# One of twelve weight pieces multiplied whole in float32 in the 64-token expert turns

## The chip, the cores and the metric

The kernel runs on one core of a Trainium2 chip. TensorE multiplies, VectorE (DVE in the profile) and ScalarE (ACT) prepare its operands, GpSimd (POOL) does little here, and SyncE (SP) issues the loads. The metric is the time of one execution in microseconds (us), as the median of several.

## The reference

Two layers of a decoder trunk, 256 tokens of width 1024, all in float32. Layer 0 mixes with RWKV-7 and a latent attention and ends in a dense SwiGLU; layer 1 mixes with two attentions and ends in a choice of 2 out of 8 experts. The change touches the experts alone:

```python
def swiglu(t, w_gate, w_up, w_down):
    return (jax.nn.silu(t @ w_gate) * (t @ w_up)) @ w_down

def moe_swiglu(t, router, w_gate, w_up, w_down):
    logits = (t @ router).astype(jnp.float32)
    top_logits, top_idx = lax.top_k(logits, TOP_K)          # TOP_K = 2
    gates = jax.nn.softmax(top_logits, axis=-1)
    combine = jnp.sum(jax.nn.one_hot(top_idx, N_EXPERTS) * gates[..., None], axis=1)
    out = jnp.zeros_like(t)
    for e in range(N_EXPERTS):                              # 8 experts of width 3584
        out = out + combine[:, e:e + 1] * swiglu(t, w_gate[e], w_up[e], w_down[e])
    return out
```

## The kernel before

**Splits.** A product in float32 accuracy is made of fp32r products. `split_raw` turns a float32 weight piece of 128x1024 into two fp32r tiles: `whi` is a rounded copy that ScalarE casts (L192), `wlo` the rest that VectorE subtracts (L193). There are four pairs of `whi`/`wlo` buffers in the expert stage, used in turn, so the fifth split after another takes its buffers and must wait until TensorE has read them.

**Turns.** The experts run in eight turns, "LSLSLSLS". The four experts with the most tokens get L turns of up to 128 tokens, the others S turns of 64. In an L turn the tokens' operand has its own high and low tile, and a product is three matmuls (high x `whi`, low x `whi`, high x `wlo`). In an S turn high and low part of 64 tokens stand side by side in one 128-column operand, so a product is two matmuls (x `whi`, x `wlo`); rows 0 to 63 of the result are those of the high part, rows 64 to 127 those of the low part, and they are added later.

**Blocks.** A turn has seven blocks of 512 of the 3584 hidden columns. A block is `gate_up` (eight pieces: four of the gate, four of the up weights, result `gu`) and `down` (four pieces, accumulated into `Y`, two banks of 512 columns). They are interleaved by one: `gate_up` of a block comes ahead of `down` of the block before it. In the turns of S, `fold` makes the hidden values: `msg` and `mhl` are copies of `gu`, four small transposing matmuls `hT` fold the two halves together, ScalarE applies silu into half of a tile also called `mhl` (L1549), VectorE multiplies (L1554), and `split_to` gives the pair `mhh` that `down` multiplies. These steps are deferred by fixed numbers of pieces (`after` and `tick`); in an ordinary S block the multiplication follows the fourth piece of the next `gate_up` and the split `mhh` the sixth.

**Order.** Each engine runs its instructions in the order in which they are written. `piece` calls `run_ahead`, which splits ahead until four pieces are ready, the current one among them. So the split of a piece is written three pieces ahead of its matmuls.

**Other work in between.** The sums of a turn are added to `h` during the next turn's first two blocks (`combine`: `yh`, `yl`, matmuls `cmb`, four additions L1604 on VectorE). In a turn's fifth and sixth `down` the tokens of the next expert are gathered (`dispatch`): VectorE makes `sel` (L1395, or L1397 for an S turn), TensorE gathers with it (`xT`).

**Loads.** The weights of a block are six loads of 1 MB, each holding two pieces (`weights`, units j = 0 to 5: 0 to 3 for `gate_up`, 4 and 5 for `down`). They go through a ring of sixteen 1 MB places, all issued on SyncE's queue. Three of the places are pairs of half-size `raw` tiles, the rest are `mraw` tiles. A place is free again when its pieces have been read.

The functions that the change touches, and their callers:

Of the kernel before, what the change touches and what calls it, by code (L numbers as in the profile page):

```python
# [28 lines left out]
NFC = DE // 512  # L29
# [9 lines left out]
PLACE = (0, 4, 1, 5, 2, 6, 3, 7)  # L39
KIND = "LSLSLSLS"  # L40
NLARGE = 4

# [66 lines left out]
def _build(tc, nc, es, I, out, dbg, upto):  # L111
# [28 lines left out]
    def ps(shape, name, tag="ps"):  # L140
        return banks[tag].tile(shape, F32, name=name, tag=tag)
# [20 lines left out]
    def load_pieces(src, n, piece, mid=None):  # L162
        raws = []
        for j in range(0, n, piece):
            raw = wraw.tile([128, 1024], F32, name="raw", tag="raw")
            w = min(piece, n - j)
            nc.sync.dma_start(raw[:, :w], src[:, j:j + w])
            raws.append(raw[:, :w])
            if len(raws) == 2 and mid is not None:
                mid()  # L170
        return raws

    def stream(src, n, piece=1024):
        raws = load_pieces(src, n, piece)

        def split(i):
            return split_raw(raws[i])
        return split
# [3 lines left out]
    def split_raw(raw):  # L182
        w = raw.shape[-1]
        p = parts_.pop(0)
        parts_.append(p)
        hi = p.tile([128, 1024], F32R, name="whi", tag="whi")
        lo = p.tile([128, 1024], F32R, name="wlo", tag="wlo")
        split_to(hi[:, :w], lo[:, :w], raw)
        return hi[:, :w], lo[:, :w]

    def split_to(hi, lo, src):
        nc.scalar.copy(out=hi, in_=src)  # L192
        nc.vector.tensor_tensor(out=lo, in0=src, in1=hi.bitcast(F32), op=OP.subtract)  # L193
# [18 lines left out]
    def gain(k, n=D, t=None, o=0, eng=None):  # L212
        g = t if t is not None else b4([128, D], "gain")
        src = I[k]
        (eng or nc.gpsimd).dma_start(g[:, o:o + n],
                                     bass.AP(tensor=src.tensor, offset=src.offset, ap=[[0, 128], [1, n]]))
        return g

    def C(k):
        for offs, t in ((_COFF, cst), (_LOFF, csl), (_KOFF, csk)):  # L220
            if k in offs:
                o, n = offs[k]
                return t[:, o:o + n]
# [9 lines left out]
    def preload(func, after=None):  # L233

        after = eps if after is None else after.bitcast(F32)
        nc.scalar.activation(dummy, after, func, bias=eps, scale=0.0)  # L236
# [38 lines left out]
    half = (slice(0, 512), slice(512, 1024))  # L275
# [291 lines left out]
    with ExitStack() as l0:  # L567
# [129 lines left out]
        Y, bonus, mv = {}, {}, {}  # L697
# [330 lines left out]
    with ExitStack() as l0:  # L1028
# [42 lines left out]
        def a8(shape, name, dt=F32):  # L1071
            return a8p.tile(shape, dt, name=name, tag="a8")
# [3 lines left out]
        t = unp.tile([128, 2, D], F32, name="un")  # L1076
# [16 lines left out]
    with l1:  # L1093
# [91 lines left out]
        def load(src, eng=None):  # L1185
            p = ring.pop(0)
            ring.append(p)
            if p is wraw:
                return stream(src, 2048)
            raw = a8([128, 2048], "mraw") if p is a8p else p.tile([128, 2048], F32, name="mraw", tag="mraw")  # L1190
            (eng or nc.sync).dma_start(raw, src)
            return lambda i: split_raw(raw[:, i * 1024:(i + 1) * 1024])
        early = []

        def load_early():
# [23 lines left out]
    t = unp.tile([128, 2, D], F32, name="un")  # L1219
# [8 lines left out]
    L, m, rank, comb, gm = (rt[:, :, i] for i in range(5))  # L1228
# [93 lines left out]
    def turns():  # L1322
# [25 lines left out]

        nc.vector.tensor_scalar(room, place, NLARGE - 0.5, 64.0, op0=OP.is_lt, op1=OP.mult)
        nc.vector.tensor_scalar(room, room, 64.0, None, op0=OP.add)  # L1350
# [9 lines left out]
    def experts(kinds, late=None, hook=None):  # L1360
# [6 lines left out]
        def after(n, f):  # L1367
            deferred.append([n, f])

        def tick():  # L1370

            for d in list(deferred):
                d[0] -= 1
                if d[0] == 0:
                    deferred.remove(d)
                    d[1]()

        def weights(e, fc, j):
            if late is None or e == 0:
                return I["moe"][e, fc, j]  # L1380
            return I["moe"][ds(turn_reg[e], 1), fc, j].rearrange("o p n -> (o p) n")
# [85 lines left out]
        units = [(0, 0, j) for j in range(4)]  # L1467
        for e in range(len(kinds)):
            for fc in range(NFC):
# [2 lines left out]
                elif e < last:  # L1472
                    units += [(e + 1, 0, j) for j in range(4)]
                units += [(e, fc, j) for j in (4, 5)]
        raws, ready = [(sp, i) for sp in early for i in range(2)], []
        del units[:len(early)], early[:]

        def load_unit(eng=None):
            sp = load(weights(*units.pop(0)), eng)
            raws.extend((sp, i) for i in range(2))  # L1480

        def run_ahead(n=1 + AHEAD):
            while len(ready) < n and (raws or units):
                if not raws:
                    load_unit()
                    if not units:
                        gf[0] = gain("final_norm", t=wraw.tile([128, D], F32, name="raw", tag="raw"), eng=nc.sync)
                sp, i = raws.pop(0)
                ready.append(sp(i))

        def piece():

            run_ahead()
            return ready.pop(0)

        def products(large, terms):

            for o, a, b, start, stop in terms:
                for i, x in enumerate(a if large else (a,)):
                    nc.tensor.matmul(o, lhsT=x, rhs=b[0], start=start and i == 0, stop=False)  # L1500
            for o, a, b, start, stop in terms:
                nc.tensor.matmul(o, lhsT=a[0] if large else a, rhs=b[1], start=False, stop=stop)  # L1502
# [32 lines left out]
        def fold(sums, end):  # L1535

            H = mt.tile([128, 4, 128], F32R, name="mhh")
            t = mt.tile([128, 512], F32, name="mhl").rearrange("p (w f t) -> p w f t", w=2, f=4)
            pt = []

            def turned(w, fs):
                if not pt:
                    pt.append(ps([128, 2, 4, 64], "hT", "hT"))
                for f in fs:
                    nc.tensor.matmul(pt[0][:, w, f, :], lhsT=sums[w][:, f * 128:(f + 1) * 128], rhs=C("fold"),  # L1545
                                     start=True, stop=True)

            def silu():
                nc.scalar.activation(t[:, 0], pt[0][:, 0], AF.Silu)  # L1549
                if end:  # L1550
                    preload(AF.Sqrt)

            def times():
                nc.vector.tensor_tensor(out=t[:, 1], in0=t[:, 0], in1=pt[0][:, 1], op=OP.mult)  # L1554

            def parts():
                split_to(H[:, :, 0:64], H[:, :, 64:128], t[:, 1])
            for i in range(4):
                after(2 if end else 2 + i, lambda i=i: turned(i // 2, range(2 * (i % 2), 2 * (i % 2) + 2)))
            for n, f in zip((3, 3, 4) if end else (7, 8, 10), (silu, times, parts)):  # L1560
                after(n, f)
            return H

        def hidden_T(sgt):
            pt = ps([128, 4, 128], "hT", "hT")
            for f in range(4):
                nc.tensor.transpose(pt[:, f, :], sgt[:, f * 128:(f + 1) * 128], ident)
            hi = mt.tile([128, 4, 128], F32R, name="mhh")
            lo = mt.tile([128, 4, 128], F32R, name="mhl")
            split_to(hi, lo, pt)  # L1570
            return hi, lo

        def down(e, fc, hd, Y, nx, every=0):
            large = kinds[e] == "L"
            turn = nx is not None and kinds[e if fc + 1 < NFC else e + 1] == "L"
            for f in range(4):
                wh, wl = piece()
                if turn and f == (3 if (e, fc) != (last, NFC - 2) else 2):
                    nx = hidden_T(nx)
                x = (hd[0][:, f, :], hd[1][:, f, :]) if large else hd[:, f, :]  # L1580
                products(large, [(Y[q], x, (wh[:, half[q]], wl[:, half[q]]), fc == 0 and f == 0, fc == NFC - 1 and f == 3)
                                 for q in range(2)])
                for _ in range(every):
                    next(side[0], None)
                tick()
            return nx
# [30 lines left out]
        hd = gate_up(0, 0)  # L1617
# [12 lines left out]
        for e in range(len(kinds)):  # L1630
            Y = [ps([128, 512], "Y", "Y") for _ in range(2)]
            for fc in range(NFC):
# [6 lines left out]
                if fc == NFC - 3 and e < last:  # L1639
                    nxt = dispatch(e + 1)  # L1640
                    side[0] = until_parts(nxt)
                    hd = down(e, fc, hd, Y, nx, 2)
                    run(side[0])
                elif fc == NFC - 2 and e < last:
                    side[0] = nxt
                    hd = down(e, fc, hd, Y, nx, 1)
                    run(nxt)
                else:
                    hd = down(e, fc, hd, Y, nx)
# [4 lines left out]

    ring[:0] = [wraw2] * NRAW2 + [a8p]
    moe = experts(KIND, slots1(), gates)
    last = 99
    for n, step in enumerate(out_):
# [147 lines left out]
```

## Time and profile before

| what | value |
|---|---|
| median of 3 runs | 1522.19 us (1521.95 to 1523.29) |
| the profiled execution: its time | 1520.67 us |
| its span, first to last instruction | 1518.7 us |
| mean granted TensorE clock | 0.989 |
| expert stage, first to last `gu` matmul | 560.7 to 1486.3 us |
| busy in the span: TensorE / VectorE / ScalarE | 1435.2 / 1243.8 / 1047.1 us |

The S turns' `down` blocks run from 705.89, 941.54, 1177.12 and 1412.77 us. A row of a timeline gives start, duration, engine, line, operation, output and inputs, shape and count; in brackets stands how long the engine was idle before it and what released it. Matmuls overlap, so their cost is read from starts, not from durations. PEclk is the granted clock as a share of the full one. A row of busy time in a stretch gives the stretch, its length, and for PE, PEld, DVE, ACT and POOL the busy time with the number of instructions.

### The profile page before, as it was taken

How to read it: one execution, taken by the hardware profiler on the slowest of the kernel's cores; microseconds unless marked ns; L12 is line 12 of the kernel's file. 1: busy time of each engine (PE TensorE's matmuls, PEld its weight loads, DVE VectorE, ACT ScalarE, POOL GpSimd, SP SyncE). 2: the span in 40 equal slices, each digit the busy share in tenths (PEclk: the TensorE clock that was granted, in tenths of full speed). 3: DMA queues.
4: the chain of work that ended last, by engine and by line, in shares of the span. 5: the costliest groups of instructions: out<-in, count | busy, mean ns of one | idle time of the engine just before them, and what ended most of it. 6: DMA issues, size and time to landing. Idle time of an engine off the chain costs nothing. (4 is left out here: it accounts for less than half of the span.)

```text
span 1518.7 us, 22486 instructions
## 1 busy us (share of the span) xinstructions
PE 1435.2 (95%) x7781; PEld 1203.5 (79%) x7781; DVE 1243.8 (82%) x1634; ACT 1047.1 (69%) x1440; POOL 86.0 (6%) x154
## 2 busy tenths in 40 slices
PE   7889999999999999999989999989999989999994
PEld 6879888998788888787778887778887778878773
DVE  6786865554586669989989989989989989988995
ACT  6645345444454568878878769878768879777894
POOL 4223110001010010000000000000000000000000
PEclk9999999999999999999999999999999999999998
DMA  8230025557554759889999989999989999998951
GB/s 305 72 109 15 1 98 184 183 188 277 170 189 139 280 188 371 336 345 393 396 368 402 357 331 388 400 380 387 372 332 367 397 399 382 361 373 332 396 233 46
DMA packets 78994, 426.85 MB, mean 281 GB/s; under 512 B 9280, under 2 KB 9552, under 8 KB 43920
## 3 DMA queue, kind: packets, MB, share of 16 engines
q1 hardware_dynamic: 78048, 422.38, 73.8%
q0 software_dynamic: 816, 2.87, 0.6%
q8 instruction: 65, 1.06, 0.3%
q14 instruction: 65, 0.53, 0.1%
HBM read 424.15 MB, written 1.05 MB: 280 GB/s over the span
## 5 line engine op out<-in xcount | busy, mean ns | idle before, releaser
L193 DVE TENSOR_TENSOR wlo<-mraw,whi 128x1024 fp32r<-128x1024 f32 x546 | 645.3, 1221 | 49.4 <-ACT whi L192 43.0
L192 ACT CAST whi<-mraw 128x1024 fp32r<-128x1024 f32 x546 | 559.9, 1050 | 118.5 <-PE Y L1500 54.8
L1500 PE MATMUL gu<-whi,x 128*128 128x512 f32 x1344 | 388.0, 397 | 0.1
L193 DVE TENSOR_TENSOR wlo<-raw,whi 128x1024 fp32r<-128x1024 f32 x242 | 291.3, 1221 | 107.7 <-ACT whi L192 100.6
L192 ACT CAST whi<-raw 128x1024 fp32r<-128x1024 f32 x242 | 250.1, 1043 | 132.6 <-PE acc L197 37.9
L1500 PEld LDWEIGHTS gu<-whi,x 128*128 128x128 f32 x1344 | 248.3, 188 | 52.6 <-DVE x L193 0.4
L1502 PE MATMUL gu<-wlo,x 128*128 128x512 f32 x896 | 282.6, 397 | 3.6 <-DVE wlo L193 2.4
L1502 PEld LDWEIGHTS gu<-wlo,x 128*128 128x128 f32 x896 | 165.0, 188 | 53.1 <-DVE wlo L193 17.8
L1500 PE MATMUL Y<-whi,mhh 128*128 128x512 f32 x448 | 171.3, 422 | 20.9 <-DVE mhh L193 20.5
L1502 PE MATMUL Y<-wlo,mhh 128*128 128x512 f32 x448 | 141.5, 397 | 0.5
L1500 PEld LDWEIGHTS Y<-whi,mhh 128*128 128x128 f32 x448 | 79.1, 190 | 43.8 <-DVE mhh L193 31.3
L1502 PEld LDWEIGHTS Y<-wlo,mhh 128*128 128x128 f32 x448 | 84.2, 190 | 23.0 <-DVE wlo L193 3.5
L196 PE MATMUL cp<-u,whi 128*128 128x256 f32 (+1 forms) x360 | 101.9, 283 | 0.0
L197 PE MATMUL cp<-u,wlo 128*128 128x256 f32 (+1 forms) x360 | 101.8, 283 | 0.0
L198 PE MATMUL cp<-u,whi 128*128 128x256 f32 (+1 forms) x360 | 101.8, 283 | 0.0
L1500 PE MATMUL Y<-whi,mhl 128*128 128x512 f32 x224 | 88.0, 393 | 0.0
L197 PEld LDWEIGHTS cp<-u,wlo 128*128 128x128 f32 (+1 forms) x360 | 68.3, 190 | 0.3
L196 PEld LDWEIGHTS cp<-u,whi 128*128 128x128 f32 (+1 forms) x360 | 68.3, 190 | 0.2
L198 PEld LDWEIGHTS cp<-u,whi 128*128 128x128 f32 (+1 forms) x360 | 68.3, 190 | 0.2
L1500 PEld LDWEIGHTS Y<-whi,mhl 128*128 128x128 f32 x224 | 42.2, 188 | 7.9
L196 PE MATMUL tp<-whi,u 128*128 128x512 f32 x96 | 40.7, 424 | 2.4 <-DVE u L193 2.4
L197 PE MATMUL tp<-whi,u 128*128 128x512 f32 x96 | 39.5, 411 | 2.2 <-DVE u L193 2.2
(425 smaller groups left out, 1977.1 us busy)
## 6 DMA issues: line engine op xcount, KB each, us to landing
mraw<-in_moe SPq DMA_DIRECT2D x272, 1024.0 KB, 7.1
raw<-in_moe SPq DMA_DIRECT2D x126, 512.0 KB, 7.3
raw<-in_ffn_gu SPq DMA_DIRECT2D x44, 512.0 KB, 3.7
raw<-in_w_in SPq DMA_DIRECT2D x38, 512.0 KB, 3.7
raw<-in_ffn_d SPq DMA_DIRECT2D x22, 512.0 KB, 3.5
raw<-in_w_out SPq DMA_DIRECT2D x16, 512.0 KB, 3.7
raw<-in_w_in SPq DMA_DIRECT2D x4, 416.0 KB, 8.6
h<-in_x SPq DMA_DIRECT2D x2, 512.0 KB, 6.0
```

The costliest lines, as they stand in the source:

```text
L192: nc.scalar.copy(out=hi, in_=src)
L193: nc.vector.tensor_tensor(out=lo, in0=src, in1=hi.bitcast(F32), op=OP.subtract)
L196: nc.tensor.matmul(o, lhsT=a[0], rhs=b[0], start=start, stop=False)
L197: nc.tensor.matmul(o, lhsT=a[1], rhs=b[0], start=False, stop=False)
L198: nc.tensor.matmul(o, lhsT=a[0], rhs=b[1], start=False, stop=stop)
L1500: nc.tensor.matmul(o, lhsT=x, rhs=b[0], start=start and i == 0, stop=False)
L1502: nc.tensor.matmul(o, lhsT=a[0] if large else a, rhs=b[1], start=False, stop=stop)
```

## The change

In S turns the second of the four `down` pieces (unit j = 4, half i = 1) isn't split. Its raw float32 tile is TensorE's moving operand, and the stationary operand is the hidden tile before its split, 128x64 float32 (`t[:, 1]`, written at L1554 and until now read by the split alone), which `fold` now returns beside `H`. The product is written to rows 0 to 63 of `Y`. It is one float32 matmul for each half of the columns, in place of two fp32r ones. That piece doesn't count among the four that `run_ahead` keeps split. It happens once in each of the 28 S blocks.

```diff
+WHOLE = (4, 1)
...
             if p is wraw:
-                return stream(src, 2048)
+                pieces = load_pieces(src, 2048, 1024)
+                return lambda i: pieces[i]
...
-            return lambda i: split_raw(raw[:, i * 1024:(i + 1) * 1024])
+            return lambda i: raw[:, i * 1024:(i + 1) * 1024]
...
         def load_unit(eng=None):
-            sp = load(weights(*units.pop(0)), eng)
-            raws.extend((sp, i) for i in range(2))
+            e, fc, j = units.pop(0)
+            raw = load(weights(e, fc, j), eng)
+            raws.extend((raw, i, kinds[e] == "L" or (j, i) != WHOLE) for i in range(2))
 
         def run_ahead(n=1 + AHEAD):
-            while len(ready) < n and (raws or units):
+            while sum(len(r) == 2 for r in ready) < n and (raws or units):
...
-                sp, i = raws.pop(0)
-                ready.append(sp(i))
+                raw, i, parts = raws.pop(0)
+                ready.append(split_raw(raw(i)) if parts else (raw(i),))
...
-            return H
+            return H, t[:, 1]
...
-                wh, wl = piece()
+                w = piece()
...
-                x = (hd[0][:, f, :], hd[1][:, f, :]) if large else hd[:, f, :]
-                products(large, [(Y[q], x, (wh[:, half[q]], wl[:, half[q]]), fc == 0 and f == 0, fc == NFC - 1 and f == 3)
-                                 for q in range(2)])
+                x = (hd[0][:, f, :], hd[1][:, f, :]) if large else hd[0][:, f, :]
+                if len(w) == 2:
+                    products(large, [(Y[q], x, (w[0][:, half[q]], w[1][:, half[q]]), fc == 0 and f == 0,
+                                      fc == NFC - 1 and f == 3) for q in range(2)])
+                else:
+                    for q in range(2):
+                        nc.tensor.matmul(Y[q][0:64], lhsT=hd[1][:, f, :], rhs=w[0][:, half[q]], start=False, stop=False)
```

TensorE, one `down` of an S turn and the start of the `gate_up` behind it, before:

```order
L1500 MATMUL Y<-whi,mhh 128x512 x2
L1502 MATMUL Y<-wlo,mhh 128x512 x2
L1500 MATMUL Y<-whi,mhh 128x512 x2
L1502 MATMUL Y<-wlo,mhh 128x512 x2
L1545 MATMUL hT<-csk,msg 128x64 x2
L1500 MATMUL Y<-whi,mhh 128x512 x2
L1502 MATMUL Y<-wlo,mhh 128x512 x2
L1545 MATMUL hT<-csk,msg 128x64 x2
```

The same place on TensorE in the changed kernel (line numbers have moved by a few):

```order
L1504 MATMUL Y<-whi,mhh 128x512 x2
L1506 MATMUL Y<-wlo,mhh 128x512 x2
L1590 MATMUL Y<-mraw,mhl 64x512 x2
L1549 MATMUL hT<-csk,msg 128x64 x2
L1504 MATMUL Y<-whi,mhh 128x512 x2
L1506 MATMUL Y<-wlo,mhh 128x512 x2
L1549 MATMUL hT<-csk,msg 128x64 x2
```

The second pair of rows on `whi` and `wlo` has become one row of two matmuls on the raw tile; nothing else on TensorE has moved.

VectorE from one `mhh` of the first S turn to the next one, and on to the `sel` of the next L expert, before:

```order
L193 TENSOR_TENSOR mhh<-mhl,mhh 128x4x64
L193 TENSOR_TENSOR wlo<-mraw,whi 128x1024 x10
L1554 TENSOR_TENSOR mhl<-mhl,hT 128x256
L193 TENSOR_TENSOR wlo<-mraw,whi 128x1024 x2
L193 TENSOR_TENSOR mhh<-mhl,mhh 128x4x64
L193 TENSOR_TENSOR wlo<-mraw,whi 128x1024 x3
L1395 TENSOR_SCALAR sel<-iota,route 128x128 x2
```

The same place on VectorE in the changed kernel:

```order
L195 TENSOR_TENSOR mhh<-mhl,mhh 128x4x64
L195 TENSOR_TENSOR wlo<-mraw,whi 128x1024 x9
L1558 TENSOR_TENSOR mhl<-mhl,hT 128x256
L195 TENSOR_TENSOR wlo<-mraw,whi 128x1024 x2
L195 TENSOR_TENSOR mhh<-mhl,mhh 128x4x64
L195 TENSOR_TENSOR wlo<-mraw,whi 128x1024 x2
L195 TENSOR_TENSOR wlo<-raw,whi 128x1024
L1398 TENSOR_SCALAR sel<-iota,route 128x128 x2
```

The ten splits between `mhh` and `mhl` are nine; two splits still stand between `mhl` and the next `mhh`, and three between that and `sel` (the third of them is now that of a later piece, from a `raw` tile).

More of the change, by code (lines that the diff above doesn't have):

```diff
@@ L1474, in experts @@
                 units += [(e, fc, j) for j in (4, 5)]
-        raws, ready = [(sp, i) for sp in early for i in range(2)], []
+        raws, ready = [(raw, i, True) for raw in early for i in range(2)], []
         del units[:len(early)], early[:]
         def load_unit(eng=None):
-            sp = load(weights(*units.pop(0)), eng)
-            raws.extend((sp, i) for i in range(2))
+            e, fc, j = units.pop(0)
+            raw = load(weights(e, fc, j), eng)
+            raws.extend((raw, i, kinds[e] == "L" or (j, i) != WHOLE) for i in range(2))
         def run_ahead(n=1 + AHEAD):
-            while len(ready) < n and (raws or units):
+            while sum(len(r) == 2 for r in ready) < n and (raws or units):
                 if not raws:
```

## The prediction

> **What bounds the kernel now.** I read the page's first part, then the time of each block of the expert stage (one query for busy time in stretches), then the timelines of single blocks, and last the clock. The profiled execution took 1520.67 us, of which the span is 1518.7; the median of the runs shown is 1522.19.
>
> ```profile
> PE 1435.2 (95%) x7781; PEld 1203.5 (79%) x7781; DVE 1243.8 (82%) x1634; ACT 1047.1 (69%) x1440; POOL 86.0 (6%) x154
> ```
>
> Over the whole span TensorE looks like the bound, but the average mixes stages. The change touches only the S turns (experts 1, 3, 5, 7). I cut the first of them into its seven blocks, each from the first `Y` matmul of one `down` to that of the next, and add the end of the last one:
>
> ```profile
> core 0: us, PE busy (x) PEld busy (x) DVE busy (x) ACT busy (x) POOL busy (x), PEclk, DMA share, GB/s
> 705.89:722.75 16.86, 15.45 (x71) 11.57 (x71) 16.86 (x19) 14.65 (x18) 0.00 (x0) 1.00 1.01 403
> 722.75:737.69 14.94, 13.94 (x64) 10.40 (x65) 14.94 (x16) 12.76 (x16) 0.00 (x0) 1.00 0.96 365
> 737.69:751.98 14.29, 13.43 (x65) 10.65 (x65) 14.29 (x15) 13.33 (x17) 0.00 (x0) 1.00 1.02 417
> 751.98:766.27 14.29, 13.43 (x65) 10.64 (x65) 14.29 (x15) 13.33 (x17) 0.00 (x0) 1.00 1.01 418
> 766.27:788.05 21.78, 18.80 (x99) 15.83 (x99) 15.22 (x17) 13.61 (x18) 0.00 (x0) 0.92 0.95 363
> 788.05:804.78 16.73, 16.73 (x80) 13.83 (x81) 16.73 (x18) 14.89 (x20) 0.00 (x0) 1.00 0.98 361
> 804.78:820.44 15.66, 15.66 (x71) 12.79 (x70) 15.66 (x16) 14.05 (x17) 0.00 (x0) 1.00 1.01 419
> ...
> 1487.43:1506.98 19.55, 12.29 (x56) 8.90 (x56) 15.05 (x21) 11.10 (x18) 0.00 (x0) 0.95 0.11 39
> ```
>
> Call the seven P0 to P6. In P0 to P3 VectorE has no idle time and TensorE has gaps, so VectorE sets the pace. In P4 the gathers of the next expert come in and neither is full. In P5 and P6 the other half of the work is already that of an L turn, and TensorE has no gap either. So a change that takes work from VectorE and gives some to TensorE can gain in four blocks of seven, and must be priced block by block.
>
> Inside an ordinary block (P2) TensorE's timeline shows the pieces. I call the four pieces of `down` d0 to d3 and the eight of `gate_up` g0 to g7:
>
> ```profile
> 737.69 0.74 PE L1500 MATMUL Y<-whi,mhh 128*128 128x512 f32 x2 [0.73 <-DVE mhh L193]
> ...
> 738.73 0.63 PE L1500 MATMUL Y<-whi,mhh 128*128 128x512 f32 x2
> ...
> 739.66 0.55 PE L1545 MATMUL hT<-csk,msg 128*128 128x64 f32 x4
> 740.02 0.71 PE L1500 MATMUL Y<-whi,mhh 128*128 128x512 f32 x2
> ...
> 744.14 0.71 PE L1500 MATMUL gu<-whi,x 128*128 128x512 f32 x2
> ```
>
> d0 starts at 737.69 after waiting for `mhh` from VectorE; d1 runs from 738.73 to 739.66, 0.93 us for four matmuls, 0.23 each; d2 starts at 740.02; g1 starts at 744.14, 6.45 us after d0.
>
> **The change, part by part.** It happens once in each of 28 blocks, on d1.
>
> *Taken from VectorE and ScalarE:* one `wlo` and one `whi`. Nine `wlo` back to back take 10.30 us, and one alone 1.22, so one costs (10.30-1.22)/8 = 1.14 us of VectorE. A `whi` is 1.05 us (the ACT rows below).
>
> ```profile
> 752.97 10.30 DVE L193 TENSOR_TENSOR wlo<-mraw,whi 128x1024 fp32r<-128x1024 f32 x9
> ```
>
> *Given to TensorE:* four fp32r matmuls of 512 columns go, two float32 ones come. The trace of before has no float32 matmul of 512 columns; the nearest has 256:
>
> ```profile
> 35.35 0.27 PE L198 MATMUL cp<-ul,whi 128*128 128x256 f32 x1
> 35.46 1.24 PE L629 MATMUL lo<-zwa,lora 128*128 128x256 f32 x5
> L629 PE MATMUL lo<-zwa,lora x16: 377/379/483, 35.5 to 39.5; 128*128 128x256 f32 x16
> ```
>
> L629 leaves 16 records for eight matmuls in the source, so a float32 matmul is two records. Five records take 1.24 us with 0.38 for the last, so they start (1.24-0.38)/4 = 0.215 us apart, against 0.11 for the fp32r one of the same width just ahead (35.35 to 35.46). At twice the columns that is 0.43 a record, 0.86 a matmul, 1.72 for d1. So d1 grows by x = 1.72-0.93 = 0.79 us. Bounds: x = 0 if the four records cost no more than fp32r records of that width, and x = 0.91 if each pass costs a full 0.23 twice over (8 x 0.23 = 1.84). I take 0.79, since L629 is the same kind at half the size. By the Trainium skill, FP8 and Floating Point Precision, section TensorE Precision Notes, true FP32 is four passes through the array; at 0.23 a pass that gives 1.84 for d1, and by it the sum below would be +8.7 us instead of +5.4; L629's records are a little faster than that.
>
> *What the gain meets in P2 and P3.* VectorE would need 14.29-1.14 = 13.15 us. But there is a second loop, through the four `whi`/`wlo` buffers: the split of g5 can't start before TensorE has read `whi` of g1, since it has the same buffer. P4's second half shows this loop alone, with VectorE waiting:
>
> ```profile
> 780.78 0.71 PE L1500 MATMUL gu<-whi,x 128*128 128x512 f32 x2
> ...
> 781.52 1.05 ACT L192 CAST whi<-raw 128x1024 fp32r<-128x1024 f32 x1 [0.33 <-PE gu L1500]
> ...
> 782.61 1.23 DVE L193 TENSOR_TENSOR wlo<-raw,whi 128x1024 fp32r<-128x1024 f32 x1 [0.15 <-ACT whi L192]
> ...
> 783.83 1.23 DVE L193 TENSOR_TENSOR wlo<-mraw,whi 128x1024 fp32r<-128x1024 f32 x1
> ...
> 784.97 0.42 DVE L1554 TENSOR_TENSOR mhl<-mhl,hT 128x256 f32<-128x256 f32 x1
> ...
> 785.30 2.35 DVE L193 TENSOR_TENSOR wlo<-mraw,whi 128x1024 fp32r<-128x1024 f32 x2
> ...
> 787.57 0.42 DVE L193 TENSOR_TENSOR mhh<-mhl,mhh 128x256 fp32r<-128x256 f32 x1
> ...
> 788.05 0.51 PE L1500 MATMUL Y<-whi,mhh 128*128 128x512 f32 x1 [0.58 <-DVE mhh L193]
> ```
>
> g1 at 780.78, its `whi` of the g5 buffer at 781.52, then VectorE in order: g5, g6, `mhl`, g7, d0, `mhh`, and TensorE starts the next d0 at 788.05: 7.27 us after g1's start. Of that row of VectorE work nothing is removed, because the dropped `wlo` (d1) stands behind `mhh`. So this loop takes 6.45+7.27 = 13.72 us in P2 before, hidden under VectorE's 14.29, and 13.72+0.79 = 14.51 after: **+0.22** each.
>
> *P1:* 14.94 now, all of it VectorE. After, VectorE needs 13.80 and the loop (g1 starts at 729.18, 6.43 after d0) 6.43+0.79+7.27 = 14.49: **-0.45**.
>
> *P0* has the sums of the L expert before it:
>
> ```profile
> 708.59 0.71 PE L1500 MATMUL Y<-whi,mhh 128*128 128x512 f32 x2
> 709.41 0.74 PE L1502 MATMUL Y<-wlo,mhh 128*128 128x512 f32 x2
> ...
> 713.11 0.71 PE L1500 MATMUL gu<-whi,x 128*128 128x512 f32 x2
> ...
> 714.35 0.39 PE L1603 MATMUL cmb<-yl,sT 128*128 128x512 f32 x1
> ...
> 716.08 0.75 DVE L1604 SCALAR_TENSOR_TENSOR h<-cmb,route,h 128x512 f32<-128x512 f32 x1
> ...
> 729.18 0.71 PE L1500 MATMUL gu<-whi,x 128*128 128x512 f32 x2
> ```
>
> `h` starts at 716.08 because VectorE was busy until then; `cmb` was done at 714.74. After, VectorE is free at 714.94. TensorE is 0.79 later, less 0.40 that d2 loses now to its late `wlo` (d2 to g1 takes 4.52 here and 4.12 in P2, 740.02 to 744.14): `cmb` ends at 715.13, and `h` starts at about 715.2. All behind it moves by **-0.88**. (The split of g5 has its `whi` by 715.3 and is no later.)
>
> *P4:* d0 runs, then TensorE waits 2.40 us for `sel`, which stands on VectorE behind `mhh` and three splits, before (d1, d2, d3) as after (d2, d3, g0). That wait stays. Behind it the chain is TensorE up to g1, and then the 7.27 above: **+0.79**.
>
> *P5 and P6:* TensorE has no gap, and its cover is VectorE's time, which shrinks: **+0.79** each.
>
> *The last S turn* has no next expert: P0 and P1 as above, three blocks of +0.22, and then a tail with d1 twice. There TensorE runs d0, d1, the transposes, and waits for ScalarE and VectorE, in a row:
>
> ```profile
> 1491.32 0.39 ACT L1549 ACTIVATE mhl<-hT 128x256 f32<-128x256 f32 x1 [0.80 <-PE hT L1545]
> ...
> 1495.90 0.73 PE L1500 MATMUL Y<-whi,mhh 128*128 128x512 f32 x2 [2.71 <-DVE mhh L193]
> ```
>
> Both d1 lie on it: 2 x 0.79 = **+1.58**. No cast leaves that row, since one split still stands between the transposes and `mhh`.
>
> *Loads:* a raw tile is freed by TensorE's d1, some 2 us later than by the split. SP's queue waits on freed tiles (562.8 us of waiting, 249 times), not on the DMA, and sixteen tiles of 1 MB are over two and a half blocks of 6 MB, so I cost this at nothing.
>
> ```profile
> SPq L1191 <- DVE wlo L193: 562.8, 249, 9.6
> ```
>
> **Sum.** A turn with a successor: -0.88-0.45+2x0.22+3x0.79 = +1.48; three of them +4.44. The last: -0.88-0.45+3x0.22+1.58 = +0.91. Together **+5.35 us**: 1526.0 on the profiled execution, 1527.5 on the median. In x the sum is 28x-16.8; it turns at x = 0.60.
>
> **The rivals.**
>
> *The relief is handed on (faster).* If splits ran far enough ahead that `mhh` never waited on a buffer, P0 and P1 would gain the whole 1.14, and P2 and P3 would fall to TensorE's own time: 13.62 us (44 matmuls at 0.23, d1 at 1.72, four groups of transposes at 0.45: 0.36 from 739.66 to 740.02 and a slower pair behind), -0.67. Sum: 3 x (-2.28-1.34+2.37) + (-2.28-2.01+1.58) = -6.5, 1515.7. It decides at the wait for `mhh` in P2: gone, this case; there, mine. For it: VectorE is full in P0 to P3. Against it: P4 shows the loop bare. The Trainium skill says so too: Perfetto Trace Analysis, section Identifying the Most-Contended Engine, has one optimize the engine of the highest occupancy first, here VectorE in those blocks; P4's VectorE, at 15.22 of 21.78, is on the chain all the same.
>
> *The clock drops go (no change).* In P4 the wait for `sel` leaves TensorE 1.17 us of work in 3.41, and then the clock is halved for the next 3.41:
>
> ```profile
> 769.87 1.16 PE L1403 MATMUL xT<-sel,un 128*128 128x128 f32 x8 [2.40 <-DVE sel L1395]
> ...
> 767.63:771.04 3.41, 1.17 (x9) 1.17 (x10) 3.41 (x5) 0.68 (x1) 0.00 (x0) 1.00 1.01 420
> 771.04:774.45 3.41, 3.41 (x14) 3.04 (x14) 1.33 (x2) 1.53 (x2) 0.00 (x0) 0.50 1.01 420
> ...
> 1242.08:1245.49 3.41, 3.41 (x14) 3.02 (x13) 1.50 (x2) 1.53 (x2) 0.00 (x0) 0.50 1.01 418
> ```
>
> That costs 1.7 us, three times. First and third lie 471.04 us apart, 138 stretches of 3.413, so they seem to follow a fixed grid, and a shift of the blocks by 1.5 us a pair could move the wait across a grid line. Without two or three of them: 1522.4 to 1524.1. Against it: the wait itself stays as long.
>
> *Float32 is dearer.* x = 0.91 gives 28 x 0.91-16.8 = +8.7: 1530.9.
>
> **How the numbers follow.** A measurement of this kernel can't tell under 0.2%, 3.0 us, from no change. The loop as summed, within 1524.5 to 1530 on its own: 0.58. The clock drops gone: 0.20. Handed on: 0.12. Dearer: 0.10. Slower by over 0.2% (above 1525.2) takes nearly all of the first and the last, 0.63; no change 0.25; faster 0.12. The range leaves out most of the faster case and what lies above the dear one: 1518 to 1531.5.
>
> **What would show it.** P2 at 14.5 us with VectorE no longer full and d0 still waiting for `mhh`; d1 at 1.72; P5 and P6 longer by 0.8 each; P0 and P1 shorter by 0.9 and 0.45. I am wrong if P2 is at 13.6 with no wait for `mhh`, if d1 is near 1.5 or less, or if the halved clock no longer shows.

## The result, and the profile after

The changed kernel takes 1541.51 us in the median (1539.99 to 1543.94, four runs), the kernel before 1522.16 on the same chip: a ratio of 1.0121, 95% interval 1.0107 to 1.0136. It is slower by 19.35 us. The forecast was slower by 5.35 us, with 1531.5 as the upper end. The profiled execution took 1542.74 us, of which its span is 1540.6.

The page's first part of the changed kernel, to be held against the same line of before:

```profile
PE 1464.3 (95%) x7781; PEld 1196.9 (78%) x7781; DVE 1223.2 (79%) x1606; ACT 1022.8 (66%) x1412; POOL 85.8 (6%) x154
```

VectorE's busy time fell by 20.6 us (28 instructions) and TensorE's grew by 29.1 at an unchanged count of matmul records: two float32 matmuls of two records took the place of four fp32r ones. 29.1 over 28 pieces is 1.04 us a piece, where 0.79 had been forecast; it is only a first hint, since the clock is in it too.

The busy time of the first S turn's blocks P0 to P2 and P4 to P6 (P3 is 14.84 like P2), of the end of the last turn, and of P4 in the second S turn (22.95 us in the third):

```profile
core 0: us, PE busy (x) PEld busy (x) DVE busy (x) ACT busy (x) POOL busy (x), PEclk, DMA share, GB/s
708.84:725.22 16.38, 15.95 (x71) 11.49 (x71) 16.00 (x18) 13.80 (x17) 0.00 (x0) 1.00 0.99 399
725.22:740.07 14.85, 14.28 (x65) 10.36 (x65) 14.27 (x15) 11.65 (x15) 0.00 (x0) 1.00 0.98 393
740.07:754.91 14.84, 14.26 (x64) 10.36 (x64) 13.59 (x14) 12.37 (x16) 0.00 (x0) 1.00 1.02 404
...
769.75:793.93 24.18, 21.22 (x99) 15.53 (x99) 13.99 (x16) 12.75 (x17) 0.00 (x0) 0.86 0.81 318
793.93:811.73 17.80, 17.80 (x81) 13.55 (x81) 16.30 (x17) 14.27 (x19) 0.00 (x0) 1.00 0.93 367
811.73:828.52 16.79, 16.79 (x71) 12.42 (x70) 15.45 (x17) 13.20 (x16) 0.00 (x0) 1.00 0.96 374
...
1504.40:1540.60 36.20, 17.43 (x56) 9.15 (x56) 13.54 (x19) 9.77 (x17) 0.00 (x0) 0.72 0.15 48
...
1010.53:1033.49 22.96, 20.01 (x98) 14.62 (x99) 13.99 (x16) 12.74 (x17) 0.00 (x0) 0.93 0.88 335
```

Against before, P0 is shorter by 0.48, P1 by 0.09, P2 and P3 are longer by 0.55 each, P4 by 2.4 in this turn and 1.2 in the others, P5 by 1.07 and P6 by 1.13. In P2 VectorE works 13.59 of 14.84 us: it isn't the bound any more, and the block is longer all the same. The relief was real and bought nothing there.

TensorE's timeline in that P2 shows d0 to d2, g1 and the next d0:

```profile
740.07 0.73 PE L1504 MATMUL Y<-whi,mhh 128*128 128x512 f32 x2 [0.57 <-DVE mhh L195]
740.64 0.62 PE L1506 MATMUL Y<-wlo,mhh 128*128 128x512 f32 x2
741.19 1.93 PE L1590 MATMUL Y<-raw,mhl 128*64 128x512 f32 x4
743.05 0.66 PE L1549 MATMUL hT<-csk,msg 128*128 128x64 f32 x4
743.52 0.71 PE L1504 MATMUL Y<-whi,mhh 128*128 128x512 f32 x2
...
747.64 0.71 PE L1504 MATMUL gu<-whi,x 128*128 128x512 f32 x2
...
754.91 0.73 PE L1504 MATMUL Y<-whi,mhh 128*128 128x512 f32 x2 [0.59 <-DVE mhh L195]
```

d0 to g1 is 747.64 - 740.07 = 7.57 us, against 6.45 before: x = 1.12, and 1.13 by P6 (16.79 - 15.66). From g1 to the next d0 it is 754.91 - 747.64 = 7.27 us, the same as the row taken from P4 of before, and d0 still waits for `mhh`. So the loop of the prediction holds to 0.01 us (7.57 + 7.27 = 14.84), and one number in it was wrong: x. The question for the experiments was where the missing 0.33 us a piece comes from. Three places can be read off: d1 starts 0.55 after the `wlo` group ahead of it, where 0.46 is usual (+0.09); it lasts 743.05 - 741.19 = 1.86 and not the forecast 1.72 (+0.14); and the transposes behind it take 743.52 - 743.05 = 0.47, against 0.36 before (+0.11).

### The profile page after: what moved, and what is told of

It reads as the page before. It is cut to its first block, busy times and chain, and to the rows that moved or that the text cites. A ratio compares the mean times of both kernels' runs of the same rounds, so it can differ in the third digit from the quotient of the medians.

```text
span 1540.6 us, 22379 instructions
## 1 busy us (share of the span) xinstructions
PE 1464.3 (95%) x7781; PEld 1196.9 (78%) x7781; DVE 1223.2 (79%) x1606; ACT 1022.8 (66%) x1412; POOL 85.8 (6%) x154
## 5 line engine op out<-in xcount | busy, mean ns | idle before, releaser
L195 DVE TENSOR_TENSOR wlo<-mraw,whi 128x1024 fp32r<-128x1024 f32 x526 | 630.1, 1223 | 75.1 <-ACT whi L194 62.5
L194 ACT CAST whi<-mraw 128x1024 fp32r<-128x1024 f32 x526 | 542.0, 1051 | 157.8 <-PE Y L1504 94.5
L195 DVE TENSOR_TENSOR wlo<-raw,whi 128x1024 fp32r<-128x1024 f32 x234 | 283.4, 1222 | 115.9 <-ACT whi L194 112.7
L194 ACT CAST whi<-raw 128x1024 fp32r<-128x1024 f32 x234 | 242.2, 1044 | 141.8 <-PE acc L199 37.9
L1504 PE MATMUL Y<-whi,mhh 128*128 128x512 f32 x392 | 153.5, 425 | 16.2 <-DVE mhh L195 15.8
L1506 PE MATMUL Y<-wlo,mhh 128*128 128x512 f32 x392 | 122.8, 395 | 0.1
L1504 PEld LDWEIGHTS Y<-whi,mhh 128*128 128x128 f32 x392 | 68.6, 190 | 40.5 <-DVE mhh L195 26.6
L1506 PEld LDWEIGHTS Y<-wlo,mhh 128*128 128x128 f32 x392 | 73.7, 189 | 18.4 <-DVE wlo L195 1.4
L1549 PEld LDWEIGHTS hT<-csk,msg 128*128 128x128 f32 x224 | 31.3, 190 | 19.4 <-ACT mhl L1528 13.8
L198 PE MATMUL tp<-whi,u 128*128 128x512 f32 x96 | 39.3, 410 | 2.4 <-DVE u L195 2.4
```

The costliest lines, as they stand in the source:

```text
L198: nc.tensor.matmul(o, lhsT=a[0], rhs=b[0], start=start, stop=False)
```

## The experiments

The question of the operand is summed up first; P2 is that of the first S turn. The edits are shown shortened, without the code around them.

| whole piece d1 | stationary columns | kind | P2, us | median, us |
|---|---|---|---|---|
| kernel before | 128 | fp32r, split | 14.29 | 1522.2 to 1522.9 |
| the change (`mhl`) | 64 | float32 | 14.84 | 1541.51 |
| e5 (`mhh`, high half) | 64 | float32 | 14.85 | 1540.07 |
| e9 (`mhh`) | 96 | float32 | 14.50 | 1529.02 |
| e1 (`mhh`) | 128 | float32 | 14.52 | 1527.66 |
| e6 (`mhl`) | 128 | float32 | 14.51 | 1528.89 |
| e2 (`mhh`, high half) | 64 | fp32r, split | 14.29 | 1523.41 |

**e1, 128 columns.** The whole piece is multiplied as float32, but with both parts of the hidden values side by side, as the split pieces have them.

```diff
-nc.tensor.matmul(Y[q][0:64], lhsT=hd[1][:, f, :], rhs=w[0][:, half[q]], ...)
+nc.tensor.matmul(Y[q], lhsT=hd[0][:, f, :].bitcast(F32), rhs=w[0][:, half[q]], ...)
```

> The changed kernel, but the whole piece is multiplied by the 128-column operand (high and low part side by side, read as float32) and written to all 128 rows of Y. In the changed kernel d1 with what it delays takes 1.13 us more than before and not 0.79. Theory A (the number of columns): a 64-column operand isn't loaded under a running 128-column matmul, nor the other way round, and the two switches cost the missing 0.34. Then x is 0.79 here, an ordinary block (P2) 14.51 us, the sum +5.4 us: 1527.5, the drops of the clock at the end included or not, up to 1530. Theory B (the kind): the change from fp32r to float32 and back costs it whatever the columns. Then nothing changes: P2 14.85, 1541.

Measured: 1527.66 us (1521.04 to 1530.36, seven runs) against 1522.85 of before, ratio 1.003 (1.001 to 1.0049). Busy time of P0, P1, P2, of P4 in the three turns with a successor, and of P6:

```profile
707.64:723.66 16.02, 15.60 (x70) 11.86 (x70) 15.91 (x18) 13.79 (x17) 0.00 (x0) 1.00 0.98 396
723.66:738.18 14.52, 13.95 (x65) 10.73 (x65) 14.17 (x15) 11.65 (x15) 0.00 (x0) 1.00 0.99 401
738.18:752.70 14.52, 13.94 (x65) 10.73 (x65) 13.60 (x14) 12.38 (x16) 0.00 (x0) 1.00 1.02 399
767.19:790.87 23.68, 20.73 (x99) 16.05 (x99) 14.00 (x16) 12.74 (x17) 0.00 (x0) 0.86 0.86 336
1005.41:1027.74 22.33, 19.33 (x98) 15.54 (x98) 13.99 (x16) 12.73 (x17) 0.00 (x0) 0.92 0.93 351
1242.19:1263.17 20.98, 17.99 (x98) 14.44 (x98) 13.99 (x16) 12.73 (x17) 0.00 (x0) 1.00 0.99 397
...
808.32:824.77 16.45, 16.45 (x71) 12.79 (x70) 15.45 (x17) 13.19 (x16) 0.00 (x0) 1.00 0.97 381
```

These are the blocks that the prediction forecast for the change itself: P0 15.98, P1 14.49, P2 14.51, P6 16.45. The piece costs x = 16.45 - 15.66 = 0.79. So float32 as such was priced rightly, and the rest lies in what e1 changed: the 64 columns, or the tile that they come from. The three P4 rows show what the clock does by itself (the seven runs go from 1521.04 to 1530.36): 23.68, 22.33 and 20.98 us for the same work, with two halved stretches, one and none.

**e2, 64 columns in fp32r.** The kernel before, with d1 split as ever, but multiplied by the 64 high columns alone; the products with the low part are left out of that piece.

```diff
-x = hd[:, f, :]                      # into Y[q]
+x = hd[:, f, 0:64] if f == 1 else hd[:, f, :]      # into Y[q][0:64] for f == 1
```

> The kernel before, all pieces split, but d1 of each S block multiplies only the 64 columns of the high part (all four matmuls fp32r); left out is the product with the low part in that piece. Theory A: the same switches without any float32, 0.34 us a block, hidden under VectorE in P0 to P3 and seen in P4 to P6 and twice in the tail: 9 x 0.34 + 2 x 0.34 = +3.7, 1526; P6 at 16.0 instead of 15.66. Theory B: no change, 1522, P6 15.66.

Measured: 1523.41 us, ratio 1.0004 (0.9994 to 1.0014). Timeline of P2:

```profile
742.24 0.62 PE L1502 MATMUL Y<-wlo,mhh 128*128 128x512 f32 x2
742.70 0.62 PE L1500 MATMUL Y<-whi,mhh 128*64 128x512 f32 x2
743.16 0.63 PE L1502 MATMUL Y<-wlo,mhh 128*64 128x512 f32 x2
743.63 0.56 PE L1545 MATMUL hT<-csk,msg 128*128 128x64 f32 x4
743.99 0.71 PE L1500 MATMUL Y<-whi,mhh 128*128 128x512 f32 x2
...
742.48 0.37 PEld L1500 LDWEIGHTS Y<-whi,mhh 128*64 128x64 f32 x2
...
743.40 0.65 PEld L1545 LDWEIGHTS hT<-csk,msg 128*128 128x128 f32 x4
```

The groups stand 0.46 to 0.47 apart through both changes of width, and the transposes take 0.36. The two rows of PEld, TensorE's loads of its stationary operand, start 0.22 and 0.23 us ahead of their matmuls. VectorE would hide a small cost in P2; in P6, where TensorE has no gap, the block takes 15.64 us against 15.66 before. So 64 columns cost nothing in fp32r, and the plain form of the theory (the width) falls: it had expected gaps here too. What was left was float32 and 64 columns together, or the `mhl` tile as the source, which e1 had changed along with the width.

**e5 and e6, the two apart.** e5 takes 64 float32 columns from `mhh`, e6 128 from `mhl`.

```diff
 e5: lhsT=hd[0][:, f, 0:64].bitcast(F32)                       # into Y[q][0:64]
 e6: lhsT=hd[1].rearrange("p f t -> p (f t)")[:, 64*f:64*f+128]  # into Y[q]
```

> The changed kernel, but the 64-column float32 operand of the whole piece is taken from the high half of mhh instead of mhl[:, 1]; the low part of the hidden values is left out of that piece. Theory C: float32 matmuls with a stationary operand of 64 instead of 128 columns cost the extra 0.33 us per whole piece, wherever the operand lies. Then x stays at 1.13: d0 to g1 in P2 7.57, P2 14.85, about 1541 us. Theory D: it is the mhl tile as the source (its own wait or its own place) that costs it. Then x = 0.80: d0 to g1 7.25, P2 14.51, about 1527 us.

> The changed kernel, but the float32 operand of the whole piece has 128 columns and still lies in the mhl tile: the 64 columns of piece 1 and the 64 behind them, into all 128 rows of Y, so that products of another piece are added to the low rows. Theory C (64 columns in float32 cost it): P2 14.51, d0 to g1 7.25, about 1527 us, as with 128 columns of mhh. Theory D (the mhl tile costs it): P2 14.85, about 1541 us.

Measured: e5 1540.07 us (ratio 1.0113, 1.0093 to 1.0133), e6 1528.89 (1.0048, 1.0032 to 1.0063). The first fence is P2 of e5, the second of e6, as busy time:

```profile
738.92:753.77 14.85, 14.27 (x65) 10.36 (x65) 13.60 (x14) 12.36 (x16) 0.00 (x0) 1.00 1.02 404
```

```profile
737.70:752.21 14.51, 13.92 (x65) 10.73 (x65) 13.60 (x14) 12.37 (x16) 0.00 (x0) 1.00 1.02 403
```

Theory C (float32 with 64 columns) gave both blocks to 0.01 us; theory D (the `mhl` tile) had them the other way round and falls.

How it costs is seen in the weight loads. First those of the changed kernel around d1, then those of e6:

```profile
740.41 0.42 PEld L1506 LDWEIGHTS Y<-wlo,mhh 128*128 128x128 f32 x2
741.19 0.19 PEld L1590 LDWEIGHTS Y<-raw,mhl 128*64 128x64 f32 x2 [0.36 <-issue]
741.67 0.14 PEld L1590 LDWEIGHTS Y<-raw,mhl 128*64 128x64 f32 x1 [0.29 <-issue]
...
743.05 0.52 PEld L1549 LDWEIGHTS hT<-csk,msg 128*128 128x128 f32 x4 [0.81 <-ACT mhl L1528]
```

```profile
738.26 0.63 PE L1506 MATMUL Y<-wlo,mhh 128*128 128x512 f32 x2
738.50 0.42 PEld L1590 LDWEIGHTS Y<-raw,mhl 128*128 128x128 f32 x2
738.73 1.88 PE L1590 MATMUL Y<-raw,mhl 128*128 128x512 f32 x4
...
740.02 0.19 PEld L1549 LDWEIGHTS hT<-csk,msg 128*128 128x128 f32 x1 [0.24 <-ACT whi L194]
740.44 0.55 PE L1549 MATMUL hT<-csk,msg 128*128 128x64 f32 x4
```

In e6 the load for d1 starts at 738.50, under the matmul before it and 0.23 ahead of its own; the load for the transposes at 740.02, 0.42 ahead. In the changed kernel d1's load starts at 741.19 and the transposes' at 743.05, both in the same moment as their matmuls: on either side of the 64-column piece nothing was loaded ahead. In e5 it is the same (load and matmul of d1 both at 740.04, of the transposes at 741.90), while e1 and e9 load ahead as e6 does, and so does e2 with its 64 columns in fp32r. A 64-column load is short (0.14 us a piece); what was lost is its cover.

By the Trainium skill, TensorE: Matmul & The Clock Gate, section Step-by-step: what each phase is for, TensorE pulls weight loads ahead of running matmuls, with conditions; the rows of e6 agree, those of the change show a place where it doesn't. By the Trainium skill, TensorEngine Tiling (Array Packing), section Key Properties, changing the tiling mode of the array drains TensorE; its section Available Configurations lists a mode of 128x64. The change agrees in sign, at 0.33 us for a switch there and back; e2 doesn't agree, since it changes the width twice at no cost. Why float32 alone loses the cover isn't shown by these runs.

**e9, 96 columns**, to see whether anything below the full width is charged.

```diff
+lhsT=hd[0][:, f, 0:96].bitcast(F32)     # into Y[q][0:96]
```

> The changed kernel with a 96-column float32 operand from mhh (its 64 high columns and 32 of the low ones, the other 32 low ones left out), into 96 rows of Y. If every operand of fewer than 128 columns is charged, P2 is 14.85, d0 to g1 7.57, about 1541 us. If the price comes only with half a stationary array or less, P2 is 14.51, d0 to g1 7.25, about 1527 us. I take the second at 0.6.

Measured: 1529.02 us (ratio 1.003, 1.0008 to 1.0052); busy time of P2:

```profile
740.02:754.52 14.50, 13.92 (x65) 10.63 (x65) 13.60 (x14) 12.36 (x16) 0.00 (x0) 1.00 1.02 407
```

96 columns cost no more than 128. Widths between 64 and 96, and below 64, weren't tried.

**e3, the tail.** The change, with the last turn's last two blocks split as before.

```diff
-raws.extend((raw, i, kinds[e] == "L" or (j, i) != WHOLE) for i in range(2))
+raws.extend((raw, i, kinds[e] == "L" or (j, i) != WHOLE or (e == last and fc > 4)) for i in range(2))
```

> The changed kernel, but the last two blocks of the last turn split all pieces. Theory A with the clock: the tail gets back two pieces of 1.13 and the 2.6 us that the halved clock took behind the last wait for mhh: -4.9, 1536.6. Rival (the clock drop in the tail has nothing to do with the whole pieces): -2.3, 1539.2, with the halved clock still there.

Measured: 1537.63 us (1536.36 to 1540.95, four runs), ratio 1.0099 (1.0075 to 1.0124), 3.9 us below the change. The stretches from the last `down` to the end of the span, and the one halved clock stretch with work in it:

```profile
1504.05:1536.80 32.75, 13.85 (x56) 10.08 (x56) 15.73 (x21) 11.66 (x19) 0.00 (x0) 0.74 0.16 53
...
1513.03:1516.44 3.41, 3.41 (x9) 2.67 (x8) 0.56 (x1) 0.00 (x0) 0.00 (x0) 0.50 0.00 0
```

The tail is 32.75 where the change has 36.20 and before 31.27. The work is that of before again, and it is still 1.48 us longer, with one halved stretch at work in it (the change has two, from 1513.30). So the two whole pieces of the tail and what the clock made of them are about 3.4 us together, and the 1.48 that is left is about what one full stretch at half the clock costs (half of 3.41 is 1.7, an estimate). Neither expectation came out whole: one halved stretch went with the pieces, the other stayed. The interval of the ratio reaches some 4 us to either side, so the time alone wouldn't tell the two apart.

**e4, another piece.** The whole piece is now g6 (the seventh of `gate_up`), with the 128-column tokens' operand, in blocks 2 to 5 alone (counted from 0; their g6 fall in P0 to P3). On VectorE g6 stands inside the row from g1 to `mhh` that closes the loop; d1 stands behind it.

```diff
-WHOLE = (4, 1)
+WHOLE = (3, 0)                          # and only where 2 <= fc <= 5
+if len(pw) == 1:
+    nc.tensor.matmul(a, lhsT=x.bitcast(F32), rhs=pw[0][:, c], start=kb == 0, stop=kb == 7)
```

> The whole piece on 128 columns is not d1 but g6, and only in gate_up of blocks 2 to 5 of an S turn, 16 in all. The dropped split then stands between that of g5 and mhh, inside the loop that the prediction named. Theory (the loop through the buffers decides): the loop is 1.14 shorter, an ordinary block falls to TensorE's own 13.8 us, P0 and P1 gain 1.1 each, P2 and P3 0.45 each: -12.4, 1510. Rival (the place in the block doesn't matter, only how much goes to which engine): P0 -0.88, P1 -0.45, P2 and P3 +0.22, so 4 x -0.89 = -3.6, 1518.6.

Measured: **1505.87 us** (1505.27 to 1507.48, four runs), ratio 0.9892 (0.9872 to 0.9912), faster than both. P0, P1, P2 and P4:

```profile
706.68:723.54 16.86, 15.89 (x70) 11.74 (x70) 16.86 (x19) 14.13 (x17) 0.00 (x0) 1.00 1.01 411
723.54:737.36 13.82, 13.82 (x65) 10.74 (x65) 13.82 (x15) 11.68 (x15) 0.00 (x0) 1.00 1.00 397
737.36:751.12 13.76, 13.76 (x65) 10.78 (x65) 13.48 (x14) 12.39 (x16) 0.00 (x0) 1.00 1.03 418
764.85:784.07 19.22, 17.14 (x100) 14.37 (x99) 14.11 (x16) 13.56 (x17) 0.00 (x0) 1.00 1.01 412
```

P1 and P2 are now TensorE's own time, with no gap left (13.82 of 13.82, 13.76 of 13.76), which is what the rival of the relief handed on had described, at 13.62. P4 is 2.6 us shorter than before, with the clock at 1.00 throughout: the splits run one piece further ahead, so `sel` stands behind two splits and not three, TensorE waits 1.50 us for it and not 2.40, and the clock isn't halved. P0 gained nothing: the splits run one piece ahead there, and d1's takes the freed place ahead of `mhh`. So 1506 instead of the expected 1510 isn't the loop's doing alone: P1 to P3 give some 2.2 us a turn (P3 is 13.73), 8.8 in all, where 8.0 was expected; P0's 4.4 didn't come, and the three P4 brought 7.7 that the expectation didn't have.

**e7, `mhh` earlier.** e1, with the split into `mhh` scheduled one piece earlier, so that on VectorE it stands ahead of d0's split.

```diff
-for n, f in zip((3, 3, 4) if end else (7, 8, 10), (silu, times, parts)):
+for n, f in zip((3, 3, 4) if end else (7, 8, 9), (silu, times, parts)):
```

> As the kernel with 128 columns of mhh (1527.66 us), but the split into mhh is scheduled one piece earlier (7, 8, 9 instead of 7, 8, 10), so that on VectorE it stands ahead of the split of d0 and not behind it. Loop theory: the way from g1 to the next d0 (7.26 us) loses the 1.15 of d0's split, and d0's second half then waits some 0.6 for that split: P2 and P3 about 14.0 instead of 14.51, P5 and P6 (no gap on TensorE) unchanged, about 1521 us in all. Rival, VectorE's or TensorE's sum alone sets P2: no change, 1527 to 1528 us.

Measured: 1523.63 us (1522.21 to 1526.42, ten runs), ratio 1.0007 (0.9997 to 1.0016), 4.0 below e1. P0, P2 and P5:

```profile
707.27:723.68 16.41, 15.34 (x71) 11.86 (x70) 16.28 (x18) 13.51 (x18) 0.00 (x0) 1.00 0.97 401
737.49:751.57 14.08, 13.92 (x65) 10.73 (x64) 13.63 (x14) 12.43 (x16) 0.00 (x0) 1.00 1.01 395
788.39:806.14 17.75, 17.61 (x81) 13.73 (x80) 17.11 (x18) 15.55 (x21) 0.00 (x0) 1.00 0.98 395
```

P2 fell from 14.52 to 14.08 (14.0 was expected), with the same work on both engines; a bound by either engine's sum, the rival, would have left it. What is left is no longer the loop: TensorE works 13.92 of 14.08 us and doesn't wait for `mhh`, only 0.16 for d0's split. P0 grew by 0.39 and P5, forecast as unchanged, by 0.30: what the earlier `mhh` pushes back on VectorE comes late there. In P0 TensorE stands 1.07 us until `yl` is written, and in P5 the `wlo` matmuls of d0 start 0.77 behind its `whi` ones, where 0.46 is usual. Some 4 of the 6.5 us expected were kept.

**e8, one block more.** e4 with g6 whole in blocks 1 to 5.

```diff
-... or (j, i) != WHOLE or not 2 <= fc <= 5
+... or (j, i) != WHOLE or not 1 <= fc <= 5
```

> As the kernel with g6 whole on 128 columns in blocks 2 to 5 (1505.87 us), but in blocks 1 to 5. The piece of block 1 then falls in P0, where VectorE has one split less ahead of mhh: P0 about 15.75 instead of 16.86 in four turns, -1.1 each, 1501.5 us. Rival: TensorE, which carries the sums of the expert before in P0, or the two h additions set its end: P0 at 16.5 or more, 1504.5 to 1506 us.

Measured: **1502.36 us** (1501.43 to 1506.76, four runs), ratio 0.9864 (0.9847 to 0.988). P0:

```profile
710.18:725.87 15.69, 15.59 (x71) 11.84 (x70) 15.69 (x18) 13.22 (x16) 0.00 (x0) 0.95 1.01 420
```

P0 is 15.69, as expected (15.75): the splits are one piece ahead from the block before on, so that VectorE has one less to do here. And this though TensorE's clock was granted at 0.95 in this record. The intervals of e4 and e8 overlap a little; the block shows the gain more plainly than the time. This is the best version found: 1.4% faster than before, from the same edit on another piece and with a full-width operand.

## Why the prediction was wrong, point by point

**The term that failed is x**, "d1 grows by x = 1.72-0.93 = 0.79 us". L629's records gave the rate of float32 rightly (0.43 us a record; e1 has 0.79 for the whole piece), but they have 128 stationary columns. The changed operand has 64, which stood in the diff, and no row of before has float32 with 64. The upper bound of 0.91 counted passes alone and left out what lies between matmuls, so the range had no room for 1.13. The rival of dearer float32 had the direction and neither the size nor the cause.

**The sum in x held.** 28x-16.8 gives +5.3 at 0.79; e1 measured +4.8. Its blocks bear that out better than its total, where luck helped: in its profiled execution the P4 blocks have three halved stretches in all, as before, only spread two, one and none. At x = 1.13 the sum gives +14.8, and that alone would be 1537.0, above the range. In the profiled executions, the span is 21.9 us longer than before, which splits so: 14.8 from the sum; 1.2 from a second halved stretch in the first P4 (24.18 against 22.96); 2.7 from the tail, 36.20 against 31.27 plus two pieces at 1.13; and 2.95 from a later start of the first S block (708.84 against 705.89), in work that the change doesn't touch, since the first `gu` matmul of the expert stage already starts at 563.61 and not 560.66. That is 21.7; the remaining 0.2 is spread over the blocks. Of the median's 19.35, the sum and the clock in P4 and the tail are 18.7, if the one profiled execution stands for the others.

**P0 and P1.** Forecast -0.88 and -0.45, measured -0.48 and -0.09, short by 0.40 and 0.36, which is the missing 0.33 and a little more; in e1 -0.84 and -0.42.

**P2 and P3.** Forecast +0.22, measured +0.55; the loop through the buffers was right: e1, e5, e6 and e9 each came out as it says, and e7, which shortened it, shortened the block.

**P5 and P6.** TensorE without a gap pays x in full: +1.07 and +1.13.

**P4.** x plus the clock. The forecast kept one halved stretch in each of the three P4; the change has two in the first. The rival in which they go was real as a mechanism (20.98 in one P4 of e1, 19.22 in e4), but didn't happen here. The Trainium skill, Perfetto Trace Analysis, section Identifying the Most-Contended Engine, would have one relieve VectorE first; P2 after (VectorE 13.59 of 14.84, and longer) goes against it in this place, and e4 shows what was wanted of that relief: work ahead of the wait, not behind it.

**The tail.** Forecast +1.58, measured +4.9: 2.26 from x and the rest with the two stretches at half the clock (e3 keeps one of them and 1.48 us), which weren't in the term.

**Loads.** Costed at nothing, and rightly: from 700 to 1500 us ScalarE's and VectorE's splits waited for a load 5.2 and 1.0 us in sum, where before it was 7.3 and 5.5. These two rows of the waits of SP's queue in the changed kernel stand for the 562.8 us of before:

```profile
SPq L1194 <- DVE wlo L195: 515.9, 226, 9.6
...
SPq L1194 <- PE Y L1590: 54.6, 18, 9.6
```

The split has 23 waits fewer, and the whole piece 18; 515.9 + 54.6 = 570.5, in a span that is longer by 21.9.

## What to carry to other kernels

Price an operation of a new kind from a row that agrees with it in shape as well as in type, the stationary width included, and where there is none, put the switch to it and back into the upper bound. Where a loop through buffers sets the pace, taking work off the busiest engine shortens that loop only if the work stands between the release that opens it and the result that closes it: with a full-width operand the same edit made P2 0.23 us longer behind that point (e1) and 0.53 shorter ahead of it (e4). In all it cost 5 us there (28 pieces) and gained 20 here (e8, 20 pieces), a good part of the 20 in P4, where the splits run further ahead of a wait. Which piece is taken out of a pipeline is a question of its own, beside how many.

## What the runs showed of the hardware

**Float32 with 64 stationary columns** loses the cover of its weight loads, 0.33 us for a switch there and back (P2 14.84 and 14.85); with 96 or 128 columns (14.50 to 14.52), or in fp32r with 64 (groups 0.46 apart), nothing is lost.

**In these blocks the halved clock stays on more readily than it comes.** Four stretches of e6, three around a P4 and one in an L turn:

```profile
1003.08:1006.49 3.41, 1.48 (x6) 0.67 (x4) 3.41 (x5) 3.41 (x5) 0.00 (x0) 1.00 0.99 407
1006.49:1009.91 3.42, 2.34 (x9) 2.21 (x10) 2.36 (x4) 0.18 (x1) 0.00 (x0) 0.50 1.03 411
1009.91:1013.32 3.41, 3.41 (x7) 1.48 (x6) 0.00 (x0) 0.00 (x0) 0.00 (x0) 0.50 0.53 208
1132.79:1136.20 3.41, 2.41 (x15) 2.15 (x16) 2.28 (x4) 0.81 (x2) 0.00 (x0) 1.00 0.99 372
```

At the full clock a stretch with 1.48 us of work in 3.41 was followed by half the clock, and one with 2.41 (in the L turn) was not. But at half the clock a stretch with 2.34 us of work was followed by another halved one, and the full clock came back after one that was full, 3.41. The change's first P4 has the same pair; this is the first of its two halved stretches, and it holds a gap:

```profile
772.60:776.02 3.42, 2.66 (x9) 2.07 (x10) 2.03 (x4) 0.00 (x0) 0.00 (x0) 0.50 0.82 340
```

A stretch needn't be full to bring the full clock back: in e1's second P4 2.85 us of work at half the clock (1008.45 to 1011.86) was enough. Nor does busy time alone decide: at the full clock 1.71 us (e1, from 766.11) was followed by half the clock and 1.58 (e1, from 1243.97) wasn't, and ahead of the first L turn, among many small matmuls, 2.46 us was (before, 552.59 to 556.00).

By the Trainium skill, TensorE: Matmul & The Clock Gate, section What's actually happening, the clock halves after an idle stretch and returns after a busy one; here a stretch that was a third busy (1.17 of 3.41, before) was idle enough to halve it. The halvings of the changed kernel in P4 and the tail begin at 772.60, 1014.95, 1253.88 and 1513.30, the later three 71, 141 and 217 stretches of 3.413 us behind the first, so the grid seems fixed. Whether a wait of 2.4 us falls into one stretch or across two then depends on where the grid meets the block: in e1's third P4 the wait, 1243.39 to 1245.80, lies across the line at 1243.97, and nothing is halved. So the same P4 took 21.0, 22.3 or 23.7 us within one execution (e1).
